# Loads tied to one another, the turns of three norms moved between products, and an S5 branch without GpSimd

## The chip, the core and the metric

The kernel runs on one core of one Trainium2 chip, in one launch. The metric is the time of an execution on the device in microseconds (us). A core has TensorE (PE in the rows: matmuls and turns, which are transposes done as matmuls), VectorE (DVE), ScalarE (ACT), GpSimd (POOL) and SyncE (SP), whose queue issues all the loads and stores here. Each engine works through its own instructions in the order in which they were written.

## The reference

One layer of an encoder over 1024 tokens of width 1024, in float32:

```python
x = layer_norm(ALPHA * x + 0.5 * swiglu(x, ffn1_w1, ffn1_w3, ffn1_w2))
proj = x @ w_in
q_lat, kv_lat, k_rope, u, g_a, g_b = split(proj)
y_a = mla_attention(q_lat, kv_lat, k_rope, ...) @ w_o_attn
y_b = s5_branch(u, f_params, b_params, d_skip, w_glu) @ w_o_ssm
x = layer_norm(ALPHA * x + (sigmoid(g_a) * y_a + sigmoid(g_b) * y_b) @ w_out)
x = layer_norm(ALPHA * x + 0.5 * swiglu(x, ffn2_w1, ffn2_w3, ffn2_w2))
ple = sigmoid(x @ ple_w_gate) * (p @ ple_w_proj)
x = layer_norm(ALPHA * x + ple)
```

`swiglu` is `(silu(x @ w1) * (x @ w3)) @ w2` with a hidden width of 2816. `s5_branch` runs a complex linear recurrence over the tokens, forwards and backwards, for 32 groups of 16 channels with 64 states each, and reads the states out with a second small matrix.

## The kernel before

Tokens stand as 8 blocks of 128 (`j`) or two halves of 512 (`h`). A float32 product is done as three: both operands are split into a high part, written by ScalarE, and a remainder, by VectorE (`split`, L63; names end in `hi`/`h` and `lo`/`l`), and `mm3` (L80) multiplies high by high, high by low and low by high, with 512 columns each. Weights come through `load_raw` (L67) into four `raw` buffers and are split into three buffers each of tags `uh` and `ul` (`wload`, L72).

**The two FFNs.** Up and down products go by seven block products in the manner of Strassen. `ffn_up` stores its seven blocks of hidden values to DRAM (`hd`). `ffn_down` (L345) works through seven stages, in the order 1, 5, 6, 3, 7, 2, 4; in each it loads six pieces of `hd` (`raw<-hd`), splits them (`hh`, `hl`) with the pieces of `w2` (`wh`, `wl`) and multiplies into `pd` or `pdy`. Its weights `w2w` and `w2e` are fetched by stage (`fetch`), and all that may be fetched early is issued as soon as its buffers are free. The residual `acc` and the norm's parameters `ln` are loaded right after.

**The norms.** In stage 4, `norm_in` (L183) takes a token block at a time: `layer_norm` (L113) sums squares on ScalarE (`scr`), takes the root, and applies the two halves of the formula with two VectorE instructions (L131 and L133). TensorE then turns the block (`tln`, L146), and `split` writes it to `xhi` and `xlo`. Turns lag the norms by three blocks (`lag`), the last norm's by two; what is left is turned by `finish`, after the first slabs of the following product have begun. A turn that is `late` goes in two tiles of four 128x128 turns through the four `pdn` buffers of PSUM; others are one tile of eight.

**Input projections.** The slabs of `w_in` (128 output columns each, 48 matmuls over both halves) follow: after the first norm the first two of four slabs of `u` (`begin`, `us[:2]`), the first half of the tokens ahead of `finish`; then the other two, six slabs of latents with the sums for their RMS norms (`pms`, `rXr`, `rXi`), and eight of the sixteen gate slabs, all under the name `pg`. `ud` holds u in DRAM; 32 loads bring it back as `U`.

**S5** (`s5_branch`, L1032) runs beside the latents and the gates. `gen` (L1249) makes, for four groups of channels, the readout weights `V`, the input weights `W` (turned on TensorE: `pw`), a Toeplitz block `K` (`pkx`, to DRAM and back as `M`) and tables `Cw`, `Sw` of cosines and sines, made from `T1` and `T2`. `scan` (L1302) multiplies `U` by `W` (`pe`), rotates by `C` and `S`, runs eight `tensor_tensor_scan` instructions into `Xr` and `Xi`, and rotates back. `read_out` (L1339) makes `py` from `M`, `Xr` and `Xi`. There are eight such iterations. GpSimd does: the products and sums of `Cw`, `Sw`, the two sums after the first rotation, and the forward half (64 partitions) of the sums after the second; VectorE does the backward half with reversed columns, and copies `bb` into `bdr`, `bdi`. In steady state 96 `pg` matmuls stand between an iteration's `pe` and the next.

**FFN2 and the end.** `first2` (L924) multiplies rows 0 and 1 of the first up products (`plain`, 96 matmuls), then calls `finish` for four blocks of the second norm, whose turns go through `tcl`, `tch`, `td`. After the third norm, `pgate` and `pproj` make the per-layer embedding, a token block at a time.

The order on each engine is set by a scheduler that works with costs of its own, subject to the data and to the pools' buffers.

Of the kernel before, what the change touches and what calls it, by code (L numbers as in the profile page):

```python
# [20 lines left out]
F32 = mybir.dt.float32  # L21
F32R = mybir.dt.float32r
# [23 lines left out]
def layer_kernel(ctx, tc, A):  # L46
# [19 lines left out]

    def load_raw(src, n=1024):  # L67
        raw = wts.tile([128, n], F32, tag="raw", bufs=RAW, name="raw")
        nc.sync.dma_start(raw, src)
        return raw  # L70

    def wload(src, tag="u", pool=None, bufs=None, n=1024):  # L72
        pool = pool or wts
        raw = load_raw(src, n)
        hi = pool.tile([128, n], F32R, tag=tag + "h", bufs=bufs, name="whi")
        lo = pool.tile([128, n], F32R, tag=tag + "l", bufs=bufs, name="wlo")
        split(raw, hi, lo)
        return hi, lo
# [104 lines left out]
    def norm_in(steps, acc, gt, bt, xT, pool, done=None, lag=3, blocks=False):  # L183


        ready = []

        def bring(late):
            j = ready.pop(0)
            if blocks:  # L190
                transpose_blocks(acc, j, xT)
            else:
                transpose_in(acc[j], j, xT, late)
            if done:
                done(j)

        def finish():
            while ready:
                bring(True)

        for j, sums in steps:
# [142 lines left out]

    def ffn_down(fp, acc, hd, w2, homes):  # L345

# [3 lines left out]
        def block(i, q):  # L350
            p, n = DUOS[q]
            t, o = (W[i], p) if p < 8 else (ends[i[0]], 3 * i[1] + p - 8)
            return t[:, o:o + n, :]

        def fetch(i):
            if i[0] not in ends:
                ends[i[0]] = homes["end", i[0]]("w2e", F32)
            W[i] = homes[i]("w2w", F32)
            for q in range(len(DUOS)):
                p, n = DUOS[q]  # L360
                nc.sync.dma_start(block(i, q), w2[i[0], i[1]][:, p:p + n, :])

        X = [pdn.tile([128, 512], F32, tag="dn", name="pd") for _ in range(4)]
        yt = []
        count = {}

# [17 lines left out]
        for i, bank, fresh, reads in stages:  # L384
            if i in want:
                fetch(want[i])
# [5 lines left out]
            for q, (p, n) in enumerate(DUOS):  # L392
                h = load_raw(hd[i - 1][q].rearrange("p a b -> p (a b)")[:, 0:n * 512], n * 512)
                w = block(right[i], q)
# [70 lines left out]
    with tc.tile_pool(name="f1", bufs=1, reuse_waits="tile") as fp:  # L465
# [80 lines left out]
        homes = {(0, 0): fx, ("end", 0): fx, (0, 1): xx, (1, 1): xx, ("end", 1): xx, (1, 0): xx}  # L546
        dn = ffn_down(fp, acc, hd, A["ffn1_w2"], homes)
        for j in range(8):
            nc.sync.dma_start(acc[j], tok(A["x"])[j])

# [3 lines left out]
        first = next(dn)  # L554
        ln = ln_params(fx("ln", F32, (128, 2, 1024)), A["ln1_g"], A["ln1_b"])
        x1T = xtiles()
        finish = norm_in(chain([first], dn), acc, *ln, x1T, fp, spill)
        us = [("w_u", m, AF.Copy, ud) for m in range(4)]
        state = begin(us[:2])
        finish()  # L560

# [362 lines left out]
    def first2():  # L924
# [33 lines left out]
        def ends():  # L958
# [12 lines left out]

    dn = ffn_down(fp, acc, hd, A["ffn2_w2"], {(0, 0): xx, ("end", 0): xx, (0, 1): xx, (1, 1): xx,
                                               ("end", 1): x16, (1, 0): x16})
    for j in range(8):
        nc.sync.dma_start(acc[j], x2d[j])
# [56 lines left out]
def s5_branch(tc, A, ud, zd, keep, pool, dram, pdn, idt):  # L1032
# [216 lines left out]
    def gen(t):  # L1249
# [47 lines left out]
        C_, S_ = tile([4, 8, 16], "Cw"), tile([4, 8, 16], "Sw")  # L1297
        cmul(C_, S_, (x(T2[0]), x(T2[1])), (y(T1[0]), y(T1[1])), g2, G)
        CS = [o.rearrange("p s a b -> p s (a b)") for o in (C_, S_)]
        return Vf, WT, M, CS  # L1300

    def scan(t, ops):  # L1302
# [20 lines left out]
        tt(t3[:, :, h], t3[:, :, h], t4[:, :, h], SUB, G)  # L1323
        X = x1, x3 = tile([4, 128], "Xr"), tile([4, 128], "Xi")
# [139 lines left out]
```

## Time and profile before

| | us |
|---|---|
| three runs: lowest, median, highest | 2364.59, 2369.57, 2371.45 |
| profiled execution | 2375.43 |
| its span, first to last instruction | 2373.6 |
| TensorE busy | 2280.4 |
| VectorE, ScalarE, GpSimd busy | 1586.0, 938.4, 390.2 |

The profile is of one execution. A row `A <- B` under waits means that A's engine sat idle until B was done. The granted clock of TensorE is given as a share: 1.00 is 2.4 GHz, 0.50 is 1.2 GHz; its mean over the span is 0.982. Durations of consecutive VectorE or TensorE instructions overlap a little, so that their starts tell the pace.

### The profile page before, as it was taken

To read this page: it belongs to the slowest core of one execution; us is meant where nothing else is said; L and a number is where in the kernel's file an instruction comes from. 1 tells how busy PE (TensorE), PEld (TensorE's weight loads), DVE (VectorE), ACT (ScalarE), POOL (GpSimd) and SP (SyncE) were. 2 spreads that over 40 slices of the span, in tenths; PEclk is the share of its full clock that TensorE was granted. 3 is DMA by queue.
4 is the path that set the end of the run, shared out by engine and by line. 5 is a ranking of instruction groups with operands and counts; after the bars stand their busy time and mean duration, and the time that the engine had idled before them with its cause. 6 is when DMAs were issued, how large, how long until landed. Compare 5 with 4: busy or idle time off the path is not lost.

```text
span 2373.6 us, 28494 instructions
## 1 busy us (share of the span) xinstructions
PE 2280.4 (96%) x10784; PEld 1876.8 (79%) x10784; DVE 1586.0 (67%) x2388; ACT 938.4 (40%) x1344; POOL 390.2 (16%) x419
## 2 busy tenths in 40 slices
PE   8999999999989989998999999989999999999897
PEld 7888888777768778886888888778888888777686
DVE  7565646665667899948688876665655646664836
ACT  5333333333432322234477871234333333233525
POOL 0000000000009455515255542000000000000000
PEclk9999999999999989998999999989999999999999
DMA  4332323932234222344100025122323327622211
GB/s 158 109 106 94 123 77 124 358 120 91 97 133 151 95 65 91 114 157 182 52 10 26 29 113 190 36 80 76 124 86 107 115 92 266 235 94 98 90 40 72
DMA packets 103899, 265.63 MB, mean 112 GB/s; under 512 B 13264, under 2 KB 27856, under 8 KB 103760
## 3 DMA queue, kind: packets, MB, share of 16 engines
q1 hardware_dynamic: 103760, 263.80, 32.3%
q8 instruction: 85, 1.39, 0.2%
q14 instruction: 54, 0.44, 0.1%
HBM read 189.33 MB, written 74.42 MB: 111 GB/s over the span
## 4 chain that ended last, share of the span: by engine, by line
PE 83%; DVE 7%; DMA 4%; issue 2%; ACT 2%; POOL 1%; SPq 0%; DVEq 0%; ACTq 0%; POOLq 0%
PE px L232 18%; PE pg L84 11%; PE py L232 9%; PE pdy L412 8%; PE pd L412 7%; PE pz L232 5%; PE pd L84 3%; PE pgate L84 3%; PE ps L84 3%; PE pov L706 2%; PE pu L270 2%; PE pg L270 2%; PE tpp L693 2%; PE pya L84 2%; DMA w2w<-in_ffn_w_dram 2%
## 5 line engine op out<-in xcount | busy, mean ns | idle before, releaser
L65 DVE TENSOR_TENSOR wlo<-raw,whi 128x1024 fp32r<-128x1024 f32 (+4 forms) x116 | 145.0, 1255 | 68.8 <-ACT whi L64 66.1
L64 ACT ACTIVATE whi<-raw 128x1024 fp32r<-128x1024 f32 (+4 forms) x116 | 112.3, 974 | 187.0 <-PE pg L84 111.4
L84 PE MATMUL pg<-xhi,whi 128*128 128x512 f32 x416 | 164.1, 395 | 0.1
L84 PE MATMUL pg<-xlo,whi 128*128 128x512 f32 x416 | 163.6, 393 | 0.3 <-DVE t L1201 0.3
L84 PE MATMUL pg<-xhi,wlo 128*128 128x512 f32 x416 | 162.9, 392 | 0.0
L412 PE MATMUL pd<-wl,hh 128*128 128x512 f32 x352 | 142.9, 406 | 6.0 <-DVE wl L65 6.0
L412 PE MATMUL pd<-wh,hl 128*128 128x512 f32 x352 | 140.9, 404 | 0.0
L412 PE MATMUL pd<-wh,hh 128*128 128x512 f32 x352 | 123.6, 404 | 7.5 <-ACT hh L64 6.6
L64 ACT ACTIVATE wh<-w2w 128x1024 fp32r<-128x1024 f32 x56 | 59.3, 1058 | 168.2 <-PE pd L412 84.2
L1232 POOL MEMSET T1r<- 128x32 f32 x1 | 0.2, 160 | 652.9 <-DMA x1d<-acc 652.9
L232 PE MATMUL py<-tch,fhl 128*128 128x512 f32 x320 | 106.0, 392 | 0.0
L412 PE MATMUL pdy<-wl,hh 128*128 128x512 f32 x264 | 104.4, 395 | 0.0
L412 PE MATMUL pdy<-wh,hl 128*128 128x512 f32 x264 | 103.9, 395 | 0.0
L65 DVE TENSOR_TENSOR hl<-raw,hh 128x1024 fp32r<-128x1024 f32 x84 | 94.9, 1132 | 11.3 <-ACT hh L64 11.2
L412 PE MATMUL pdy<-wh,hh 128*128 128x512 f32 x264 | 100.0, 396 | 0.0
L232 PE MATMUL px<-td,thi 128*128 128x512 f32 x320 | 98.8, 390 | 0.0
L64 ACT ACTIVATE fhl<-raw 128x512 fp32r<-128x512 f32 x40 | 25.3, 633 | 179.9 <-PE px L232 177.3
L65 DVE TENSOR_TENSOR wl<-w2w,wh 128x1024 fp32r<-128x1024 f32 x56 | 68.4, 1221 | 39.1 <-ACT wh L64 38.9
L680 POOL TENSOR_SCALAR P<-P,sm 128x1024 f32<-128x1024 f32 x64 | 74.8, 1170 | 117.1 <-DVE sm L679 98.4
L65 DVE TENSOR_TENSOR pt<-tpp,pt 128x512 fp32r<-128x512 f32 x128 | 85.6, 684 | 11.7 <-ACT pt L64 10.3
L84 PEld LDWEIGHTS pg<-xhi,whi 128*128 128x128 f32 x416 | 78.5, 189 | 17.2 <-issue 1.0
L84 PEld LDWEIGHTS pg<-xlo,whi 128*128 128x128 f32 x416 | 78.6, 189 | 16.8 <-DVE xlo L65 0.8
(431 smaller groups left out, 6395.0 us busy)
## 6 DMA issues: line engine op xcount, KB each, us to landing
raw<-in_ffn_w_dram SPq DMA_DIRECT2D x86, 512.0 KB, 3.7
raw<-hd SPq DMA_DIRECT2D x70, 512.0 KB, 3.3
hd<-c SPq DMA_DIRECT2D x88, 256.0 KB, 3.6
w2w<-in_ffn_w_dram SPq DMA_DIRECT2D x32, 512.0 KB, 8.6
hd<-s SPq DMA_DIRECT2D x60, 256.0 KB, 3.3
rawx<-in_xT_dram SPq DMA_DIRECT2D x16, 256.0 KB, 6.4
w2e<-in_ffn_w_dram SPq DMA_DIRECT2D x8, 512.0 KB, 8.8
acc<-in_x_dram SPq DMA_DIRECT2D x8, 512.0 KB, 8.8
```

Source lines behind the costliest of these rows:

```text
L64: S.activation(hi, src, AF.Copy)
L65: V.tensor_tensor(out=lo, in0=src, in1=hi.bitcast(F32), op=ALU.subtract)
L84: PE.matmul(out, lhsT=a, rhs=b, start=(n == 0), stop=(n == last))
L232: PE.matmul(out, lhsT=x[:, ks], rhs=y[:, k, :], start=(first and n == 0), stop=(n == 11), skip_group_check=True)
L270: PE.matmul(o, lhsT=x[:, ks], rhs=b[y][:, k, :], start=(i == 0 and k == 0 and m == 0), stop=(i == 1 and k == 3 and m == 2), skip_group_che ...
L412: PE.matmul(P[t], lhsT=x[:, ts], rhs=y[:, ws], start=(fresh and p + a == 0 and m == 0), stop=(p + a == NP - 1 and m == 2), skip_group_chec ...
L680: G.tensor_scalar(out=P, in0=P, scalar1=sm, scalar2=1.0, op0=ALU.mult, op1=ALU.mult)
L693: PE.transpose(tp[:, k * 128:k * 128 + 128], P[:, (q * 4 + k) * 128:(q * 4 + k) * 128 + 128], idt)
L706: PE.matmul(p[:, 0:256], lhsT=vt[:, k, c0:c0 + 128], rhs=pt[k // 4][b][:, k % 4, :], start=(k == 0 and b == 0), stop=(k == 7 and b == 1))
L1232: G.memset(T[0][:, :, 0], 1.0)
```

## The change

Six parts:

1. **Tied loads.** In `ffn_down`, each fetch of `w2` is issued behind a load of `hd`: the next stage's weights after this stage's third piece. The first `hd` piece of a stage is loaded ahead, at the end of the stage before; `acc` is loaded in stages 1 and 5, and `ln` behind the eighth last `hd` load. The tie is one of order on SP's queue, not a wait for the data.
2. **First norm.** The lag is four. Four slabs of `u` for the first half of the tokens (`pu`, 96 matmuls) stand ahead of `finish`, whose 32 turns come all after them; then the four slabs for the second half. The fourth slab's weights use buffers of tag `v`.
3. **u before S5.** So all of `u` is stored (8 stores `ud<-ou`) before the latents.
4. **S5 without GpSimd.** `Cw`, `Sw` and all sums go to VectorE in full width; ScalarE copies the forward rows of `Xr`, `Xi` and, reversed, the backward rows, and copies `bb` into `bdr`, `bdi`. `Vi` is made with a negated `c`, which takes away one negation per iteration. The making of `T1`, `T2` and the RMS work stay on GpSimd.
5. **first2.** `finish(2)` after row 0, and again between the parts of row 1.
6. **Third norm.** The lag is four, and `finish` comes when the gate products reach block 4.

```diff
-    def ffn_down(fp, acc, hd, w2, homes):
+    def ffn_down(fp, acc, x0, hd, w2, homes, hs):
...
+        def behind(load):
+            if hs:
+                with tc.issue_after(hs[-1].ins):
+                    load()
+            else:
+                load()
...
-            if i in want:
+            if i == 1:
                 fetch(want[i])
...
-                h = load_raw(hd[i - 1][q].rearrange("p a b -> p (a b)")[:, 0:n * 512], n * 512)
+                if q == 0:
+                    h = ahead or hload(i, 0)
+                else:
+                    h = hload(i, q)
+                if q == len(DUOS) - 1 and i != 4:
+                    ahead = hload(follows[i], 0)
+                if q == 2 and i != 4 and follows[i] in want:
+                    fetch(want[follows[i]])
+                if q == 4 and i in (1, 5):
+                    for j in range(4):
+                        behind(lambda: nc.sync.dma_start(acc[j + (i == 5) * 4], x0[j + (i == 5) * 4]))
...
-        us = [("w_u", m, AF.Copy, ud) for m in range(4)]
-        state = begin(us[:2])
-        finish()
+        us = [wload(A["w_u"][m]) if m < 3 else wload(A["w_u"][m], "v", fp, 4) for m in range(4)]
+        for h in range(2):
...
+            for w, p in zip(us, ps):
+                up(p, w, x1T, h)
+            if h == 0:
+                finish()
...
-        for row, s in ((0, s1), (1, s2)):
-            for _ in plain(X2b, w, 0, row, s[:, l]):
-                pass
-        finish()
+        for _ in plain(X2b, w, 0, 0, s1[:, l]):
+            pass
+        finish(2)
+        for _ in plain(X2b, w, 0, 1, s2[:, l]):
+            finish(2)
...
-        cmul(C_, S_, (x(T2[0]), x(T2[1])), (y(T1[0]), y(T1[1])), g2, G)
+        cmul(C_, S_, (x(T2[0]), x(T2[1])), (y(T1[0]), y(T1[1])), g2, V)
...
-        tt(t1[:, :, h], t1[:, :, h], t2[:, :, h], ADD, G)
+        tt(t1[:, :, h], t1[:, :, h], t2[:, :, h], ADD, V)
...
-            tt(o[fw], x[fw], y[fw], op, G)
-            tt(o[bw, :, ::-1], x[bw], y[bw], op, V)
+            tt(x, x, y, op, V)
+            S.activation(o[fw], x[fw], AF.Copy)
+            S.activation(o[bw, :, ::-1], x[bw], AF.Copy)
```

**SP's queue at the end of FFN1's up products.** Before (w2w, w2e: weights of the down product; hd: stores and loads of the hidden values):

```order
107 L361 DMA w2w<-in_ffn_w_dram 128x1024 x4
108 L361 DMA w2e<-in_ffn_w_dram 128x1024
109 L361 DMA w2e<-in_ffn_w_dram 128x512
110 L69 DMA raw<-hd 128x1024
111 L361 DMA w2e<-in_ffn_w_dram 128x1024
112 L361 DMA w2e<-in_ffn_w_dram 128x512
113 L361 DMA w2w<-in_ffn_w_dram 128x1024 x8
114 L320 DMA hd<-s_2788 128x512
115 L361 DMA w2e<-in_ffn_w_dram 128x1024
116 L361 DMA w2e<-in_ffn_w_dram 128x512
117 L361 DMA w2w<-in_ffn_w_dram 128x1024 x4
118 L361 DMA w2e<-in_ffn_w_dram 128x1024
```

With the change:

```order
107 L367 DMA w2w<-in_ffn_w_dram 128x1024 x4
108 L367 DMA w2e<-in_ffn_w_dram 128x1024
109 L367 DMA w2e<-in_ffn_w_dram 128x512
110 L367 DMA w2e<-in_ffn_w_dram 128x1024
111 L367 DMA w2e<-in_ffn_w_dram 128x512
112 L69 DMA raw<-hd 128x1024
113 L367 DMA w2w<-in_ffn_w_dram 128x1024 x4
114 L323 DMA hd<-s_2788 128x512
115 L323 DMA hd<-s_2787 128x512
116 L420 DMA acc<-in_x_dram 128x1024 x3
```

Before, the weights of three stages (twelve `w2w`, six `w2e`) stand ahead of the last stores of `hd` (`s_2787`) and of everything behind them; now those of two, and the third set and half of `acc` follow stage 1's loads.

**ScalarE at the end of FFN1's down product.** Before:

```order
278 L64 ACTIVATE whi<-raw 128x1024
279 L64 ACTIVATE xhi<-tln 128x8x128
280 L121 ACTIVATE scr,ln_4510<-acc,ln_4509 128x1024
281 L64 ACTIVATE xhi<-tln 128x8x128
282 L121 ACTIVATE scr,ln_4549<-acc,ln_4548 128x1024
283 L121 ACTIVATE scr,ln_4588<-acc,ln_4587 128x1024
284 L123 ACTIVATE ln_4510<-ln_4511 128x1
285 L64 ACTIVATE whi<-raw 128x1024 x2
```

With the change:

```order
279 L64 ACTIVATE whi<-raw 128x1024
280 L64 ACTIVATE xhi<-tln 128x8x128
281 L123 ACTIVATE scr,ln_4498<-acc,ln_4497 128x1024
282 L64 ACTIVATE whi<-raw 128x1024 x2
283 L123 ACTIVATE scr,ln_4537<-acc,ln_4536 128x1024
284 L64 ACTIVATE whi<-raw 128x1024
285 L123 ACTIVATE scr,ln_4576<-acc,ln_4575 128x1024
286 L64 ACTIVATE xhi<-tln 128x8x128
```

The second `xhi<-tln` of each piece is that of block 3, the last one that the first half of the tokens needs. Before it stood behind one `scr`; now it stands behind three `scr` and three `whi<-raw`. On VectorE, `xlo` of block 3 likewise stands behind three `wlo<-raw` and the first norm instruction of blocks 4, 5 and 6.

**VectorE in one S5 iteration, the part behind the scans.** Before:

```order
835 L1066 TENSOR_TENSOR Wr<-Wr,v_7046 128x512
836 L1327 SCALAR_TENSOR_TENSOR Xi<-r_4788,t_7018 128x128 x4
837 L1066 TENSOR_TENSOR t_7016<-Xr,Cw 128x512
838 L1066 TENSOR_TENSOR t_7019<-Xr,Sw 128x512
839 L1066 TENSOR_TENSOR v_7046<-PW_4779,bb_re 128x512
840 L1066 TENSOR_TENSOR t_7017<-Xi,Sw 128x512
841 L1066 TENSOR_TENSOR t_7018<-Xi,Cw 128x512
842 L1066 TENSOR_TENSOR Wi<-Wi,v_7046 128x512
843 L1066 TENSOR_TENSOR Xr<-t_7016,t_7017 64x4x128
844 L1066 TENSOR_TENSOR Xi<-t_7018,t_7019 64x4x128
```

With the change:

```order
901 L1104 TENSOR_TENSOR t_7296<-Xr,Cw 128x512
902 L1104 TENSOR_TENSOR t_7299<-Xr,Sw 128x512
903 L1104 TENSOR_TENSOR t_7297<-Xi,Sw 128x512
904 L1104 TENSOR_TENSOR t_7298<-Xi,Cw 128x512
905 L65 TENSOR_TENSOR wlo<-raw,whi 128x1024
906 L1104 TENSOR_TENSOR v_7328<-PW_4966,bb_re 128x512
907 L1104 TENSOR_TENSOR t_7296<-t_7296,t_7297 128x512
908 L1104 TENSOR_TENSOR Sw<-T2r,T1i 128x512
909 L1104 TENSOR_TENSOR t_7298<-t_7298,t_7299 128x512
910 L1104 TENSOR_TENSOR Cw<-T2r,T1r 128x512
911 L1104 TENSOR_TENSOR Wi<-Wi,v_7328 128x512
912 L1104 TENSOR_TENSOR Cw<-Cw,v_7329 128x512
```

Two half-width sums (64x4x128) became two full ones (`t<-t,t`, 128x512), and the products and sums of `Cw` and `Sw` (six per iteration) now stand among VectorE's instructions. On TensorE the `pg` matmuls between one iteration's `pe` and the next went from 96 to 83 in most iterations, one has 78; behind the last `pe` 41 stand ahead of the readout, where 48 stood.

## Rows read from the trace of the kernel before

**Rows 1.** Busy time by stretch: length, then each engine (count), granted clock, DMA share, GB/s.
```profile
426.50:468.87 42.37, 42.37 (x184) 34.14 (x182) 30.09 (x32) 11.08 (x14) 0.00 (x0) 1.00 1.03 413
...
470.97:477.80 6.83, 6.08 (x14) 4.79 (x15) 6.12 (x9) 4.75 (x5) 0.00 (x0) 0.50 1.03 419
...
2037.69:2041.10 3.41, 3.41 (x9) 2.63 (x9) 2.64 (x3) 3.14 (x4) 0.00 (x0) 0.50 1.03 422
827.85:836.20 8.35, 5.11 (x26) 4.65 (x26) 8.18 (x10) 0.00 (x0) 8.19 (x9) 0.80 0.21 65
853.39:866.92 13.53, 7.72 (x33) 6.91 (x33) 11.94 (x15) 3.28 (x6) 7.36 (x8) 0.62 0.22 76
1583.72:1597.37 13.65, 11.51 (x33) 8.69 (x34) 12.24 (x21) 3.34 (x5) 0.00 (x0) 0.50 0.00 1
672.44:686.01 13.57, 3.22 (x13) 2.96 (x13) 13.57 (x36) 6.31 (x13) 0.40 (x1) 0.62 0.41 153
2236.29:2253.00 16.71, 10.95 (x42) 7.81 (x41) 15.87 (x39) 10.05 (x17) 0.00 (x0) 0.80 0.38 126
```

**Rows 2.** Waits of PE over 468 to 475 us: line, releaser, us in total, times, longest.
```profile
PE pd L412 <- ACT hh L64: 2.9, 1, 2.9
```

**Rows 3.** Waits of PE over 2030 to 2040 us.
```profile
PE pd L412 <- ACT hh L64: 3.8, 1, 3.8
```

**Rows 4.** DMA issues over 430 to 475 us: count, KB each, median us to landing.
```profile
w2w<-in_ffn_w_dram SPq DMA_DIRECT2D x12, 512.0 KB, 9.3
```

**Rows 5.** Waits of PE over 672 to 700 us.
```profile
PE tln L146 <- DVE ln L128: 10.4, 1, 10.4
```

**Rows 6.** ACT groups over 672 to 700 us: count, busy us, mean ns, idle before.
```profile
L121 ACT ACTIVATE scr<-acc,ln 128x1024 bf16<-128x1024 f32 x3 | 3.4, 1136 | 0.0
L64 ACT ACTIVATE xhi<-tln 128x512 fp32r<-128x512 f32 x6 | 3.3, 601 | 11.0 <-PE tln L146 11.0
L64 ACT ACTIVATE whi<-raw 128x1024 fp32r<-128x1024 f32 x2 | 2.0, 1046 | 0.0
```

**Rows 7.** DVE over 672 to 690 us, in time: start, us, line, tile, count.
```profile
674.15 1.28 DVE L131 SCALAR_TENSOR_TENSOR acc<-acc,ln,ln 128x1024 f32<-128x1024 f32 x1
...
676.79 2.34 DVE L65 TENSOR_TENSOR wlo<-raw,whi 128x1024 fp32r<-128x1024 f32 x2
```

**Rows 8.** Waits of PE over 800 to 875 us.
```profile
PE pw L1270 <- DVE Wr L1066: 5.1, 1, 5.1
PE py L1346 <- DVE Xr L1066: 2.9, 1, 2.9
PE pw L1270 <- DVE Wi L1066: 1.4, 2, 0.8
PE py L1344 <- DMA M<-kd: 1.0, 1, 1.0
```

**Rows 9.** DVE groups over 875 to 1025 us: count, busy us, mean ns, idle before.
```profile
L1066 DVE TENSOR_TENSOR Vi<-Vi,v 128x512 f32<-128x512 f32 x5 | 7.0, 1394 | 0.0
...
L1066 DVE TENSOR_TENSOR t<-pe,Cw 128x508 f32<-128x508 f32 x10 | 6.7, 673 | 1.7 <-PE pe L1311 1.7
```

**Rows 10.** DVE over 824 to 828 us, in time.
```profile
824.94 0.68 DVE L1066 TENSOR_TENSOR t<-Xi,Sw 128x512 f32<-128x512 f32 x1
825.54 0.68 DVE L1066 TENSOR_TENSOR t<-Xi,Cw 128x512 f32<-128x512 f32 x1
```

**Rows 11.** The stretch 875 to 1025 us, columns as in Rows 1.
```profile
875.00:1025.00 150.00, 150.00 (x896) 128.15 (x896) 142.10 (x196) 44.20 (x55) 78.64 (x60) 1.00 0.32 99
```

**Rows 12.** PE groups over 875 to 1025 us: count, busy us, mean ns.
```profile
L84 PE MATMUL pg<-xhi,wlo 128*128 128x512 f32 x166 | 64.9, 391 | 0.0
```

**Rows 13.** Waits of PE over 1550 to 1595 us.
```profile
PE tln L162 <- DVE tcl L65: 4.1, 2, 3.6
```

**Rows 14.** Waits of PE over 2230 to 2280 us.
```profile
PE pgate L84 <- DVE wlo L65: 2.3, 2, 1.5
PE pgate L84 <- ACT whi L64: 2.0, 1, 2.0
```

More of the change, by code (lines that the diff above doesn't have):

```diff
@@ L65, in split, with load_raw @@
         V.tensor_tensor(out=lo, in0=src, in1=hi.bitcast(F32), op=ALU.subtract)
-    def load_raw(src, n=1024):
+    def load_raw(src, n=1024, note=None):
         raw = wts.tile([128, n], F32, tag="raw", bufs=RAW, name="raw")
-        nc.sync.dma_start(raw, src)
+        dma = nc.sync.dma_start(raw, src)
+        if note is not None:
+            note.append(dma)
         return raw
@@ L195, in bring, with finish @@
                 done(j)
-        def finish():
-            while ready:
+        def finish(n=8):
+            while ready and n:
                 bring(True)
+                n -= 1
         for j, sums in steps:
@@ L360, in fetch, with hload @@
                 p, n = DUOS[q]
-                nc.sync.dma_start(block(i, q), w2[i[0], i[1]][:, p:p + n, :])
-        X = [pdn.tile([128, 512], F32, tag="dn", name="pd") for _ in range(4)]
-        yt = []
-        count = {}
+                behind(lambda: nc.sync.dma_start(block(i, q), w2[i[0], i[1]][:, p:p + n, :]))
+        def behind(load):
[4 more added lines that the diff above has]
+                load()
+        X = [pdn.tile([128, 512], F32, tag="dn", name="pd") for _ in range(4)]
+        follows = {1: 5, 5: 6, 6: 3, 3: 7, 7: 2, 2: 4}
+        ahead = None
+        def hload(i, q):
+            n = DUOS[q][1] * 512
+            return load_raw(hd[i - 1][q].rearrange("p a b -> p (a b)")[:, 0:n], n, hs)
         def add(out, j, n, ps, first, last):
@@ L402, in ffn_down @@
                 held.append((p, n, hh, hl, wh, wl))
+                if i == 4 and 0 < q < 5:
+                    yield q - 1, sums[q - 1]
                 if i == 4 and q == 4:
@@ L546, in layer_kernel @@
         homes = {(0, 0): fx, ("end", 0): fx, (0, 1): xx, (1, 1): xx, ("end", 1): xx, (1, 0): xx}
-        dn = ffn_down(fp, acc, hd, A["ffn1_w2"], homes)
-        for j in range(8):
-            nc.sync.dma_start(acc[j], tok(A["x"])[j])
+        hs = []
+        dn = ffn_down(fp, acc, tok(A["x"]), hd, A["ffn1_w2"], homes, hs)
         def spill(j):
@@ L554, in layer_kernel @@
         first = next(dn)
-        ln = ln_params(fx("ln", F32, (128, 2, 1024)), A["ln1_g"], A["ln1_b"])
+        with tc.issue_after(hs[-8].ins):
+            ln = ln_params(fx("ln", F32, (128, 2, 1024)), A["ln1_g"], A["ln1_b"])
         x1T = xtiles()
-        finish = norm_in(chain([first], dn), acc, *ln, x1T, fp, spill)
-        us = [("w_u", m, AF.Copy, ud) for m in range(4)]
-        state = begin(us[:2])
-        finish()
+        finish = norm_in(chain([first], dn), acc, *ln, x1T, fp, spill, 4)
+        us = [wload(A["w_u"][m]) if m < 3 else wload(A["w_u"][m], "v", fp, 4) for m in range(4)]
+        for h in range(2):
+            if h == 0:
+                ps = [t[:, c:c + 512] for t in [pup.tile([128, 1024], F32, tag="up", name="pu") for _ in range(2)]
+                      for c in (0, 512)]
+            else:
+                ps = [pdn.tile([128, 512], F32, tag="dn", name="pu") for _ in range(4)]
+            for w, p in zip(us, ps):
+                up(p, w, x1T, h)
+            if h == 0:
+                finish()
+            for m, p in enumerate(ps):
+                o = fp.tile([128, 512], F32, tag="s", bufs=2, name="ou")
+                S.activation(o, p, AF.Copy)
+                nc.sync.dma_start(ud[m][:, h * 512:h * 512 + 512], o)
     def latents(ev, tp):
@@ L970, in layer_kernel @@
     acc = [fa.tile([128, 1024], F32, tag="a", bufs=8, name="acc") for _ in range(8)]
[L972 to L975, printed above, removed]
+    hs = []
+    dn = ffn_down(fp, acc, x2d, hd, A["ffn2_w2"], {(0, 0): xx, ("end", 0): xx, (0, 1): xx, (1, 1): xx,
+                                               ("end", 1): x16, (1, 0): x16}, hs)
     first = next(dn)
-    gt, bt = ln_params(x16("ln", F32, (128, 2, 1024)), A["ln3_g"], A["ln3_b"])
+    with tc.issue_after(hs[-8].ins):
+        gt, bt = ln_params(x16("ln", F32, (128, 2, 1024)), A["ln3_g"], A["ln3_b"])
     x3T = [[f(n) for _ in range(2)] for f, n in ((xx, "xhi"), (x16, "xlo"))]
-    finish = norm_in(chain([first], dn), acc, gt, bt, x3T, fp, lag=2)
+    finish = norm_in(chain([first], dn), acc, gt, bt, x3T, fp, lag=4)
     gt, bt = ln_params(x16("ln", F32, (128, 2, 1024)), A["ln4_g"], A["ln4_b"])
```

23 lines of the change are left out of this document (12 added, 11 removed).

## The prediction

> **What bounds the kernel now.** I read the span and the busy times first: TensorE is busy for 2280.4 of 2373.6 us, so the kernel is bound by its matmuls, and only what TensorE loses can be won. Then I took TensorE's waits stretch by stretch, and the granted clock of the same stretches. [rows 1] is to be read this way: where a stretch has the clock 0.50 throughout, TensorE was at 1.2 GHz, and half of its busy time there is lost on top of the idle time. In every one of these stretches the clock fell after an idle gap, never in the full ones (the first row: 42.37 of 42.37 us busy, clock 1.00). So an idle gap costs twice, and a change that moves no matmul away must show as smaller gaps. The losses that the change touches, idle and clock:
>
> - Entry of FFN1's down product: 2.9 us [rows 2], then 6.08 us busy at half clock, of which half is lost [rows 1]: 2.9 + 3.0 = 5.9. FFN2's: 3.8 [rows 3] and 3.41 / 2 [rows 1]: 5.5.
> - After the first norm: 10.4 idle [rows 5], then 3.22 us busy at half clock [rows 1]: 12.0.
> - S5's start: 5.1 + 2.9 + 1.4 + 1.0 = 10.4 idle [rows 8]. Two stretches of [rows 1] show its clock: 8.35 us at 0.80 means 3.3 us at half clock, all of it busy, 1.7 lost; 13.53 at 0.62 means 10.3 at half clock, with all 7.72 busy us in it, 3.9 lost. Together 16.0.
> - FFN2's first products: 4.1 idle [rows 13] and 11.51 / 2 = 5.8 from the clock [rows 1]: 9.9.
> - Behind the third norm: 16.71 - 10.95 = 5.8 idle, and 0.20 x 2 x 16.71 = 6.7 us at half clock, mostly busy, some 2.8 lost [rows 1]: 8.6.
>
> **The change part by part.**
>
> *Tied loads.* At 426.5 to 468.87 the DMA share is 1.03 at 413 GB/s [rows 1]: everything issued there stands in line, and a weight block takes 9.3 us to land [rows 4]. The late `hh` of [rows 2, 3] waits for `hd` loads at the end of this line. Before, three sets of weights, `ln` and `acc` stood ahead of them (12 x 0.5 MB in `w2w` alone); the order now puts two sets and half of `acc` there: about 5.5 + 2 MB instead of 8.3 + 4 + 1, some 5.8 MB less, 14 us at 413 GB/s. The last `hd` piece, 3 us late, comes early. The third set then comes under the first stages, where the products last longer than its 7 us. I take the whole 5.9 + 5.5 = **-11.4**; bounds -11.4 and, if the last stores of `hd` set the time and not the line, -5.
>
> *First norm.* Here the order speaks against a gain. The 96 `pu` matmuls may start when block 3 is in `xhi` and `xlo`. Count from T, the end of the last `pd`. ScalarE has two `whi`, whose buffers the last products free, one `scr`, one `whi`, one `scr` ahead: 3 x 1.05 + 2 x (1.14 + 0.19 for reading the sum), then `xhi`, about 1.0 [rows 6]: T + 6.8. VectorE has three norm instructions of 1.28 and three `wlo` of 1.17 ahead [rows 7], plus a last sum and small ones, about 1.2, then `xlo` with 1.2: T + 9.7. The second matmul of `pu` already reads `xlo`. TensorE has block 3's eight turns to do, 1 us, so it idles about 8.7 instead of 10.4, with the clock lost as before and more busy time in it (2.4 instead of 1.6). The 32 turns behind come in eight late tiles; each takes ScalarE 0.60 [rows 6] and four buffers are there, so with the copy of the last `pu` ahead the last `xhi` is written some 5.4 us after that product, while the turns themselves take about 4 (13 matmuls in 3.22 us at half clock is 0.12 each at full, [rows 1]): another 1.5. Sum -1.7 + 0.8 + 1.5, about **+1**; bounds -12 (gap gone) and +4. The stores and loads of `u` that are moved ahead of the latents have some 100 us until the first `pe`, and cost nothing as long as the latents' 200-odd matmuls cover them.
>
> *S5 without GpSimd.* Beside GpSimd, VectorE's sums with two SBUF inputs take 1.39 us; those that read `pe` from PSUM take 0.67 at all times [rows 9]; where GpSimd is still, two-input ones take 0.68 and start every 0.60 [rows 10]. So the 30 products and sums of an iteration after the change cost 18 us, the eight scans 2.7, `wlo` and `K` 2.4: about 23 us. TensorE's iteration: 32 matmuls of each kind make one, so 166 in 150 us [rows 12] are 5.2 iterations of 29 us; at 42.37 / 184 = 0.23 each [rows 1], 13 fewer between make it 26. VectorE, busy for 142.1 of 150 us before [rows 11], gets air although its list is longer. With that the late `Wr`, `Xr` and `Wi` of [rows 8] come in time: behind the first `pe` the order leaves 65 `pg` and 28 small matmuls, about 19 us, before `Xr` is read; VectorE and ScalarE need about 15.5. At the end it gets worse: 41 instead of 48 `pg` cover the last chain (10 products and sums at 0.60, scans 2.7, two copies of 0.6 at the end: 11 us against 9.4), about +1. I leave 1.5 for waits that stay. Sum -16.0 + 1 + 1.5 = **-13.5**; bounds -17 and, if only the waits for GpSimd's own results go, -4.
> The Trainium skill (SBUF — State Buffer, section Who interferes with whom) says that a VectorE instruction with two SBUF inputs and a GpSimd instruction that reads SBUF block each other for a whole instruction, while one with at most one SBUF input is left alone. The trace agrees: 1.39 against 0.67. By that rule no such pair ever ran together, and moving GpSimd's half over gives up no overlap.
>
> *first2.* Four turns at a time between parts of plain products give `tcl` and `td` a time of 36 matmuls, 8 us, to be written. The gaps go, and the clock with them: 9.9 less some 0.4 that stays: **-9.5**; bounds -11 and -4.
>
> *Third norm.* Turning block 3 behind the last `pd`, with three `whi` in a row, leaves one wait of about 2.2 us for the second `wlo` (VectorE writes it behind `xlo` and a norm instruction) where 2.3 + 2.0 stood [rows 14]; the 32 late turns cost about 2 as above, the clock about 1. 8.6 becomes 5.2: **-3.5**; bounds -8.6 and +2.
>
> Matmuls are neither added nor taken away. Sum: -11.4 + 1 - 13.5 - 9.5 - 3.5 = -36.9. The profiled execution, 2375.43 us with 1.8 outside its span, lies 5.9 above the median of 2369.57. From 2375.4 it goes to 2338.5, which for the median means **2332.7**.
>
> **The rivals.**
>
> *A: VectorE becomes the bound of S5 (slower).* If its sums are slow for another reason than GpSimd, the moved ones are slow too. Before, an iteration cost VectorE 142.1 / 5.2 = 27.5 us; without the negation, the half-width sums and the copies about 20.5. Ten more at 1.39 make 34.4 against TensorE's 26: 8.4 lost in each of eight iterations, +67, and the start's 13.5 isn't won. 2332.7 + 13.5 + 67 = 2413. It decides as soon as the mean pace of the 30 passes 0.70 us. For it: VectorE was near full. Against: [rows 9, 10]. Chance 0.04.
>
> *B: the first norm's gap closes.* If block 3 is written before the queued work that I count, 12 us go instead of +1: 2320. Against it stands the order on ScalarE and VectorE. Chance 0.12.
>
> *C: S5 keeps its late start.* The copies of `Xr`, `Xi` stand on ScalarE behind table loads and an `og` that waits for a slab's end; if they come 3 to 5 us later than I count, the gaps and the clock loss stay, and only 4 is won: 2342. Together with a first2 that keeps its clock loss: 2348. Chance 0.16.
>
> *D: the down entries wait on for the last `hd` stores*, and the ties do little: -5 instead of -11.4, so 2339. Chance 0.10.
>
> *E: most gaps return elsewhere*, as the next late thing takes each place (`raw` loads, `M`, the first norm): under 7 us are left, about 2366. Chance 0.04.
>
> **How the numbers follow.** The forecast gets what remains, 0.54, and is 2332.7. Its own bounds are not all met at once: about 12 either way. B and full gains reach 2314, C with a bad first norm 2354; these are the ends of the range, and A, E and corners lie outside it. A measurement of this kernel can tell about 0.3%, 7 us, from no change. Faster by more: forecast, B, C, D, 0.92. Within it: E, 0.04. Slower: A, 0.04.
>
> **What would show it.** Right: no wait over 1 us and a clock of 1.00 at the two down entries, with a DMA share there well below 1.03 in the last 20 us; a gap of 8 to 9 us behind the first norm, ended by `xlo`; S5 iterations of about 26 us in which VectorE's two-input sums take 0.68; first2 without the stretch at 0.50. Wrong: sums on VectorE above 0.70 in pace with GpSimd still, waits for `Xr` of several us, or a first norm under 3 us idle.

## The result, and the profile after

The change took the kernel from 2367.93 us (median of four runs on the same chip, 2364.59 to 2371.45) to **2340.28 us** (2339.93 to 2342.82): a ratio of 0.9885, 95% interval 0.9868 to 0.9903. The forecast was 2332.7, its range 2314 to 2354. The sign and the range held. The sum of terms came close partly by luck: one wait that no step had foreseen ate what other places gave beyond their forecast.

The profiled execution of after took 2340.56 us, at its own median, with a span of 2338.7; that of before, 2375.43, stood 7.5 above this median of 2367.93. So between the two profiles 34.9 us went, between the medians 27.7. TensorE's busy time went from 2280.4 to 2260.9, its mean clock from 0.982 to 0.991. Six places that both traces have, each the start of the same wait on TensorE (the last is the span's end), show where; the lead is how much earlier after reaches the place:

| place | before | after | lead | gained since the place above |
|---|---|---|---|---|
| FFN1's down product, `pd<-wl,hh` | 641.84 | 636.20 | 5.6 | 5.6 |
| behind S5, first wait at `pglu<-zs,whi` | 1061.56 | 1054.65 | 6.9 | **1.3** |
| attention, `pov<-pt,vt` | 1223.92 | 1211.37 | 12.6 | 5.6 |
| start of FFN2, `pu<-xah,whi` | 1554.19 | 1541.58 | 12.6 | 0.0 |
| FFN2's down product, `pd<-wl,hh` | 2205.67 | 2176.54 | 29.1 | 16.5 |
| end of the span | 2373.6 | 2338.7 | 34.9 | 5.8 |

The stretch of the first norm, `u` and S5, on which parts 2 to 4 of the change work, gained next to nothing. TensorE's waits of after, four stretches one behind the other (columns as in [rows 2]):

```profile
PE pu L86 <- ACT xhi L64: 5.3, 1, 5.3
PE pu L86 <- DVE xlo L65: 2.5, 1, 2.5
PE tln L148 <- DVE xlo L65: 0.7, 1, 0.7
...
PE pms L625 <- DVE rXr L65: 12.3, 1, 12.3
...
PE py L1390 <- DMA M<-kd: 1.3, 1, 1.3
PE pw L1315 <- DVE Wr L1104: 0.8, 1, 0.8
...
PE pgate L86 <- DVE wlo L65: 2.2, 1, 2.2
PE tln L148 <- DVE xlo L65: 1.5, 2, 1.1
PE pgate L86 <- ACT whi L64: 0.4, 1, 0.4
```

The first two stand for [rows 5], and come to 7.8 us where the forecast said 8.7; the third is a wait at the late turns. The two rows with `M` and `Wr` are all that is left of the four in [rows 8]. The row between is new: 12.3 us at the first `pms`, the sum over squares of a latent slab for its RMS norm. Before has no wait there. The stretches of after by engine (columns as in [rows 1]):

```profile
448.40:468.40 20.00, 20.00 (x88) 16.22 (x87) 15.60 (x16) 5.62 (x8) 0.00 (x0) 1.00 0.96 379
...
780.00:798.00 18.00, 5.65 (x15) 3.98 (x14) 8.64 (x14) 4.86 (x7) 11.66 (x40) 0.62 0.07 29
...
830.00:1020.00 190.00, 188.71 (x1158) 161.43 (x1157) 168.90 (x303) 81.99 (x125) 6.93 (x18) 1.00 0.33 98
...
1560.00:1600.00 40.00, 40.00 (x203) 33.35 (x203) 26.35 (x37) 12.87 (x17) 0.00 (x0) 1.00 0.16 54
...
1988.90:2008.90 20.00, 20.00 (x87) 16.21 (x87) 15.60 (x16) 5.62 (x8) 0.00 (x0) 1.00 0.97 374
```

Over the 20 us up to the place in each down product where before waited for `hh` (first and fifth row), TensorE is full at clock 1.00, and no wait for `hh` follows. The DMA share there is 0.96 and 0.97, little below the 1.03 of [rows 1]: the queue is still nearly full, and what changed is the order on it. ScalarE writes the `hh` that before waited for 13 us earlier, first in before, then in after:

```profile
471.04 0.63 ACT L64 ACTIVATE hh<-raw 128x512 fp32r<-128x512 f32 x1 [1.31 <-DMA raw<-hd]
...
458.10 0.61 ACT L64 ACTIVATE hh<-raw 128x512 fp32r<-128x512 f32 x1
```

The turns of first2 (fourth row), which [rows 1] had at 0.50, run full at 1.00. S5 (third row) runs at 1.00 with 1.3 us idle in 190, and GpSimd is busy for only 6.9 us of it. The second row is the new loss: 12.35 idle, then 5.65 us busy, of which 5.1 us are at half clock, so 2.6 more: 15.0 in all. What stands behind it, followed back through after, engine by engine (start, us, line, tile, count, idle before and releaser):

```profile
726.93 0.42 SPq L1090 DMA_DIRECT2D c_re<-in_c_re_dram  x1
727.89 0.43 SPq L1194 DMA_DIRECT2D t<-in_lam_re_dram  x1
...
734.88 0.26 POOL L1104 TENSOR_TENSOR t<-t 128x32 f32<-128x32 f32 x1 [34.77 <-DVE t L1104]
...
791.41 0.24 POOL L1104 TENSOR_TENSOR Xr<-Xr,t 128x32 f32<-128x32 f32 x1
...
791.69 0.63 ACT L617 ACTIVATE rt<-og 128x512 f32<-128x512 f32 x1 [21.44 <-POOL Xr L1104]
...
788.94 0.72 DVE L1104 TENSOR_TENSOR Cw<-T2r,T1r 128x512 f32<-128x512 f32 x1 [13.18 <-POOL T2r L1104]
...
792.13 0.68 DVE L65 TENSOR_TENSOR rXr<-rt,rt 128x512 fp32r<-128x512 f32 x1
...
792.87 0.80 PE L625 MATMUL pms<-rXr,ones 128*128 128x512 f32 x1 [12.35 <-DVE rXr L65]
```

SP issues the loads of S5's parameters at 727 to 728; GpSimd starts the tables `T1`, `T2` at 735 and needs 57 us for them; their scratch is tagged `Xr`, and so is the buffer that the RMS work takes next; ScalarE's `rt<-og`, VectorE's `rXr` and TensorE's `pms` follow within 2 us of the last table instruction. The same rows of before:

```profile
686.84 0.45 SPq L1052 DMA_DIRECT2D c_re<-in_c_re_dram  x1
688.10 0.48 SPq L1156 DMA_DIRECT2D t<-in_lam_re_dram  x1
...
704.33 0.26 POOL L1066 TENSOR_TENSOR t<-t 128x32 f32<-128x32 f32 x1 [17.57 <-DVE t L1066]
...
764.85 0.63 ACT L577 ACTIVATE rt<-og 128x512 f32<-128x512 f32 x1 [7.51 <-POOL Xr L1066]
```

and before's instructions on the tile `pms` (count, shortest, median and longest in ns, first and last start):

```profile
L585 PE MATMUL pms<-rXr,ones x2: 392/396/401, 774.9 to 797.8; 128*128 128x512 f32 x2
```

The parameters were issued 40 us earlier, the tables began 31 and ended 27 us earlier. ScalarE waited for the scratch there too, 7.5 us, but TensorE had other work and came to this `pms` at 774.9, 10.05 us behind `rt<-og`, which needs 1.18 to get there (791.69 to 792.87 in after). So the slack was 8.9 us; TensorE comes 5.6 us later in after (780.5), and 26.8 - 8.9 - 5.6 is the wait of 12.3. These rows were in the trace of before, and the forecast did not use them.

On SP's queue the parameter loads wait for nothing of their own. They stand behind the stores `ud<-ou`, and SP's waits from 680 to 740 us in after are mostly those of these stores for `ou` (39.7 us). That the loads stand there because of the memory of `u`'s buffers is an inference; C, D and E change the buffers and see where the loads go.

### The profile page after: what moved, and what is told of

Same layout as the page of the kernel before. It is cut to its first block, busy times and chain, and to the rows that moved or that the text cites. A ratio compares the mean times of both kernels' runs of the same rounds, so it can differ in the third digit from the quotient of the medians.

```text
span 2338.7 us, 28503 instructions
## 1 busy us (share of the span) xinstructions
PE 2260.9 (97%) x10784; PEld 1862.5 (80%) x10784; DVE 1547.1 (66%) x2416; ACT 968.9 (41%) x1417; POOL 269.5 (12%) x339
## 4 chain that ended last, share of the span: by engine, by line
PE 48%; DVE 4%; ACT 2%; issue 1%; DMA 0%; POOL 0%; SPq 0%; DVEq 0%; ACTq 0%
PE px L235 9%; PE py L235 5%; PE pd L441 4%; PE pdy L441 4%; PE pd L86 3%; PE pgate L86 3%; PE ps L86 3%; PE pz L235 2%; PE pov L746 2%; PE tpp L733 2%; PE pya L86 2%; PE pyb L86 2%; PE pq L86 1%; PE pu L273 1%; PE pg L273 1%; PE pg L86 1%
## 5 line engine op out<-in xcount | busy, mean ns | idle before, releaser
L65 DVE TENSOR_TENSOR wlo<-raw,whi 128x1024 fp32r<-128x1024 f32 (+4 forms) x116 | 139.0, 1203 | 64.6 <-ACT whi L64 61.9
L86 PE MATMUL pg<-xhi,whi 128*128 128x512 f32 x352 | 139.0, 395 | 0.0
L86 PE MATMUL pg<-xlo,whi 128*128 128x512 f32 x352 | 138.5, 394 | 0.0
L86 PE MATMUL pg<-xhi,wlo 128*128 128x512 f32 x352 | 138.4, 393 | 0.0
L249 DVE TENSOR_TENSOR c<-raw 128x512 f32<-128x512 f32 x40 | 27.5, 688 | 93.9 <-PE px L235 93.9
L86 PE MATMUL ps<-k,qh 96*128 96x512 f32 (+1 forms) x256 | 84.3, 408 | 3.2 <-ACT P L718 1.8
L441 PEld LDWEIGHTS pd<-wl,hh 128*128 128x128 f32 x352 | 66.3, 188 | 24.1 <-DVE wl L65 9.1
```

Of the source, the lines that this page charges most:

```text
L65: V.tensor_tensor(out=lo, in0=src, in1=hi.bitcast(F32), op=ALU.subtract)
L86: PE.matmul(out, lhsT=a, rhs=b, start=(n == 0), stop=(n == last))
L249: V.tensor_tensor(out=c[:, r], in0=r2[:, l], in1=r2[:, r], op=ALU.add)
L441: PE.matmul(P[t], lhsT=x[:, ts], rhs=y[:, ws], start=(fresh and p + a == 0 and m == 0), stop=(p + a == NP - 1 and m == 2), skip_group_chec ...
```

## The experiments

Ratios are against runs of before on the same chip; the medians of before lay between 2368.26 and 2369.49. The expectations speak of `Xr` and `pms` as above.

### What the wait at `pms` consists of

**A. First product of the tables on GpSimd.**

```diff
-        cmul(C_, S_, (x(T2[0]), x(T2[1])), (y(T1[0]), y(T1[1])), g2, V)
+        cmul(C_, S_, (x(T2[0]), x(T2[1])), (y(T1[0]), y(T1[1])), g2, G if t == 0 else V)
```

> Edit: Cw and Sw of the first S5 iteration go back to GpSimd; all else as in the change. Theory M (the S5 parameters arrive about 40 us later than before because the second half of u still holds buffers whose place the S5 tiles take; so GpSimd's tables end about 27 us later): VectorE no longer waits for the tables, but ScalarE's squares of the latents share buffers with the tables' scratch, so the wait of 12.4 us moves from the first pms pair to the second, to about 8 to 12 us: 2338 to 2342 us. Rival Q (only the place of Cw in VectorE's queue delays rXr): the wait and the clock loss behind it go: about 2325 us.

Measured: 2347.08 us (2341.12 to 2353.78), 0.9914 [0.9891, 0.9937]. That is 6.8 above the change: TensorE waits 13.9 us at the same `pms`, and 4.2 us for `Xr` at S5's end, which the change does not have. VectorE around the end of the first wait:

```profile
792.72 1.53 DVE L65 TENSOR_TENSOR rXr<-rt,rt 128x512 fp32r<-128x512 f32 x1 [16.00 <-POOL Xr L1104]
794.18 1.76 DVE L619 TENSOR_TENSOR rt<-rt,rt 128x512 f32<-128x512 f32 x1
```

`Cw` no longer stands ahead of `rXr`, and `rXr` comes no earlier: it waits for the scratch itself. So it was not VectorE's order; and the wait did not pass to a later `pms` either, as I had thought the other outcome would be. GpSimd now makes part of `Cw` between its last table instructions, which ends the tables 1 us later. With GpSimd multiplying beside them, these two instructions take 1.53 and 1.76 us where after has 0.68 for the same.

**B. The tables on VectorE.** `T1` and `T2` are made with `V` in place of `G`.

> Edit: the tables T1 and T2 and the powers they need are made on VectorE instead of GpSimd; parameters arrive as late as in the change. Theory M: some 100 small instructions of 0.2 to 0.3 us, about 20 to 25 us on VectorE where GpSimd took 50 (735 to 792); rXr comes near 780 and the wait shrinks from 12.4 to 0 to 5 us: 2326 to 2333 us. Rival: VectorE is too full there and the wait stays over 8 us: 2337 us or more.

Measured: 2340.04 us, 0.9886 [0.9871, 0.9901], no change against after. The wait at `pms` is gone, and two others stand in its place:

```profile
PE py L1392 <- ACT Xr L1382: 6.1, 2, 5.9
PE pg L86 <- ACT og L479: 5.4, 1, 5.4
```

A faster maker of the tables takes the wait away, which says that their end set it; but the loss returns at 811 us (`og`) and at S5's end, 1018 us (`Xr`). The expectation had the wait and the time fall together, or neither. That VectorE is then too full is my reading, not shown.

**C. Three slabs of u, and no buffer of the FFN in the second half.** The fourth slab goes with the latents; results leave through the raw weight buffers.

```diff
-        us = [wload(A["w_u"][m]) if m < 3 else wload(A["w_u"][m], "v", fp, 4) for m in range(4)]
+        us = [wload(A["w_u"][m]) for m in range(3)]
...
-                o = fp.tile([128, 512], F32, tag="s", bufs=2, name="ou")
+                o = wts.tile([128, 1024], F32, tag="raw", bufs=RAW, name="raw")
...
+    project(sp, [("w_u", 3, AF.Copy, ud)])
```

> Edit: the first norm is covered by three slabs of u instead of four, their results leave through raw buffers, and the fourth slab comes with the latents, so that no buffer of the first FFN is held by u's second half. Theory M: the S5 parameters are issued some 20 us earlier, the tables end before VectorE asks for them, and the 12.4 us wait at pms goes with its clock loss of about 2.6: 2325 us, or up to 2329 if the fourth slab's weights come 2 to 4 us late. Rival Q: Cw still stands ahead of rXr, and the wait stays: about 2340.

Measured: 2325.58 us (2324.49 to 2328.68), 0.9827 [0.9810, 0.9843]: 14.7 below after, where the wait and its clock are worth 15.0. SP and GpSimd:

```profile
687.42 5.76 SPq L600 DMA_DIRECT2D ud<-raw  x3
693.23 0.42 SPq L1091 DMA_DIRECT2D c_re<-in_c_re_dram  x1
...
701.77 0.26 POOL L1105 TENSOR_TENSOR t<-t 128x32 f32<-128x32 f32 x1 [7.49 <-DVE t L1105]
```

The parameters are issued 34 us earlier, the tables start 33 us earlier, and TensorE has no wait at `pms`. It has another of 4.8 us instead, for the fourth slab's `whi`, with a stretch at half clock behind it (0.92 over 700 to 745 us). That 14.7 equals the price of the wait so nearly is therefore chance: the first norm's waits fell from 8.5 to 6.8 us too, and S5's own (`M`, `Wr` and, at its end, `Xi`, 2.9 us) are gone.

**D and E. Which buffer holds the parameters.** In D the change has only its results moved to the raw buffers, in E only the fourth slab's weights moved (C with the results back in tag `s`). D:

```diff
-                o = fp.tile([128, 512], F32, tag="s", bufs=2, name="ou")
+                o = wts.tile([128, 1024], F32, tag="raw", bufs=RAW, name="ou")
```

> The change with one edit: the results of u on the way out go through the raw weight buffers in place of the buffers of S5's parameters; the fourth slab's weights stay where the change has them (the buffers tagged v). Theory, the v buffers of the fourth slab hold the parameters too: they are still issued late (near 725 us), the pms wait stays at 9 to 13 us, about 2337 to 2341 us. Rival, the buffers of the results alone hold them: parameters near 690 us, no pms wait, about 2326 us as the run with three slabs and free buffers gave.

> As the run with three slabs and free buffers, but the results of u go out through the two buffers tagged s, as the change has it; so only the fourth slab's v buffers are taken away. With the run before it, this tells which of the two holds the S5 parameters. Theory, each of the two holds them by itself: the parameters come only behind the sixth store of u, near 715 us (the changed kernel 727, the run with both freed 693), the tables end some 10 us earlier than in the change, and a wait at or behind the first pms of 1 to 5 us is left: about 2330 us (2325 to 2335). Rival, the v buffers alone hold them: parameters near 693 us, no wait, about 2326 us or, since the latents' first weights are loaded earlier, 2319.

Measured, D: 2351.47 us, 0.9928 [0.9911, 0.9945]; E: 2336.49 us (2335.11 to 2337.36), 0.9869 [0.9842, 0.9896]. TensorE's waits in D:

```profile
PE pms L625 <- DVE rXr L65: 11.6, 1, 11.6
PE pg L86 <- ACT whi L64: 9.9, 1, 9.9
```

SP and ScalarE in E, in time, and TensorE's wait there:

```profile
717.11 0.32 SPq L600 DMA_DIRECT2D ud<-ou  x1
718.27 0.46 SPq L1091 DMA_DIRECT2D c_re<-in_c_re_dram  x1
...
784.26 0.63 ACT L617 ACTIVATE rt<-og 128x512 f32<-128x512 f32 x1 [16.82 <-POOL Xr L1105]
```

```profile
PE pms L625 <- DVE rXr L65: 13.2, 1, 13.2
```

In both the parameters stay late: in D `c_re` is issued at 722.7, but the load of `lam_re`, from which the tables start, only behind the last store at 728.3 (727.9 in after); in E `c_re` is issued at 718.3, against 693.2 in C. Each of the two tags holds them by itself, and only freeing both helps. My times were off in both. In D the results take raw buffers that the latents' first weights had, hence 9.9 us more at `pg`. In E the tables end 7.4 us earlier than in after, but with some 40 matmuls less ahead of it TensorE also comes to `pms` 8.3 us earlier (772.2 in place of 780.5), so the wait is as long as it was. What counts is the distance between the two, which I had not subtracted.

**F. The change with u as before**: two slabs ahead of the first norm, the others behind it, lag three; all other parts as changed.

> The change with the projection of u as the kernel before has it (two slabs ahead of the first norm, the others in the late turns as before); the tied loads, the S5 part, first2 and the third norm stay as changed. Theory, the four other parts add up and only the new order of u costs: about 2319 us (2315 to 2324), from the time of before less 10.3 (tied loads), 16.5 (first2 and third norm) and 22.3 (S5), each as its single run gave it. The S5 parameters are issued near 685 us, the wait at the first pms of S5 (12.35 us in the changed kernel) is gone, the first norm's gap is 10.4 us with the clock window behind it as before. Rival, the parts take from one another and the order of u is not what ate the gain: 2330 us or more, with gaps elsewhere.

Measured: **2322.90 us** (2322.29 to 2324.74), 0.9803 [0.9789, 0.9818]. The wait at `pms` is gone, `c_re` is issued at 679.61, and the first norm's wait is the old one:

```profile
PE tln L148 <- DVE ln L130: 10.3, 1, 10.3
```

So parts 2 and 3 of the change, taken together, cost 17.4 us (19 by the ratios).

### What the other parts are worth

**G. S5's part alone, on the kernel before.**

> Edit: the kernel before with the S5 part of the change alone (Cw, Sw and all sums on VectorE, copies on ScalarE). The forecast's term: the waits for Wr, Xr, Wi go with the clock loss, 13.5 us less than before: about 2354. Rival A (VectorE's sums stay slow without GpSimd and it becomes the bound): at or above 2368. Rival Q: Cw on VectorE waits for GpSimd's tables here too, and holds back rXr by several us: 2358 to 2368.

Measured: 2345.97 us (2339.37 to 2352.68), 0.9909 [0.9885, 0.9933], 22.3 less than before; its runs differ by 13 us, and the interval is about 6 us either way. From 700 to 1030 us TensorE is busy for 330.00 of 330 us at clock 1.00 and waits for nothing that the profile lists, so all of the 16.0 that the forecast had found there is gone. The start of the attention also lost less, though nothing in it was edited: its stretch in the table above, 162.4 us long in before, lasts 155.5 here, and the wait for `ckl` is 4.0 us in place of 6.4.

**H. The loads as before, in the changed kernel.**

> Edit: the change with the loads of both down products as before (all weights as early as their buffers allow, then acc and ln). The forecast's term: 11.4 us are given back, 2.9 and 3.8 us of waiting for hh and the clock loss behind them, so about 2351 us. Rival: the entries were won by something else, the waits stay away: about 2340.

Measured: 2350.56 us (2348.09 to 2354.75), 0.9925 [0.9906, 0.9944], 10.3 more than the change. Both waits of [rows 2, 3] are back, and the clock with them (0.83 over 470 to 480 and over 2014 to 2024 us):

```profile
PE pd L415 <- ACT hh L64: 2.8, 1, 2.8
...
PE pd L415 <- ACT hh L64: 3.6, 1, 3.6
```

**I. first2 and the third norm as before, in the changed kernel.**

> Edit: the change with first2 as before (all four turns after both rows) and the third norm's lag at two again. The two stand 450 us apart, so that the trace reads each by itself. The forecast's terms: the first products of FFN2 lose 9.5 us again (a stretch at 0.50 with some 11 us busy, gaps of 5 us), the end of the third norm 3.5 (5.8 us idle instead of 2 to 4): about 2353 us. Rival: the waits were tied to the late S5 or to the loads: 2340 to 2345.

Measured: 2356.82 us (2355.11 to 2357.95), 0.9949 [0.9933, 0.9965], 16.5 more than the change. The waits of [rows 13, 14] return, and the clock behind them (columns of [rows 2], then of [rows 1]):

```profile
PE tln L164 <- DVE tcl L65: 4.1, 2, 3.6
...
PE pgate L86 <- DVE wlo L65: 2.3, 2, 1.6
PE pgate L86 <- ACT whi L64: 2.0, 1, 2.0
```

```profile
1571.00:1585.00 14.00, 10.60 (x31) 7.97 (x32) 13.50 (x23) 3.93 (x6) 0.00 (x0) 0.51 0.00 0
2220.00:2235.00 15.00, 9.51 (x34) 6.99 (x34) 13.80 (x34) 7.96 (x14) 0.00 (x0) 0.72 0.48 140
```

G, H and I add up to 22.3 + 10.3 + 16.5 = 49.1; F, which has all three, is 46.6 below its before. So these parts take little from one another, as far as G's spread lets one say.

### What is left, and a faster version

**J. Block 3 first.** In the changed kernel the splits of slabs 2 to 4 are put behind block 3's `xhi` and `xlo` in the order.

```diff
+        a, v = splits
+        us = [wload(A["w_u"][0])]
+        with tc.issue_after(a.ins), tc.issue_after(v.ins):
+            us += [wload(A["w_u"][m]) if m < 3 else wload(A["w_u"][m], "v", fp, 4) for m in range(1, 4)]
```

> Edit: the splits of the second to fourth slab's weights are ordered behind those of token block 3. Theory of the order (xhi and xlo of block 3 stand behind three whi and three wlo): the idle time behind the first norm falls from 8.6 to about 5 us: 2336 us. Rival: the second slab's wlo then comes late, or the norm instructions alone hold xlo: idle time within 1 us of 8.6, 2340 us.

Measured: 2338.37 us (2337.39 to 2340.99), 0.9874 [0.9854, 0.9894]; 1.9 less than the change, though the runs of the two overlap. The waits behind the norm:

```profile
PE pu L88 <- ACT xhi L66: 2.4, 1, 2.4
PE pu L88 <- DVE xlo L67: 2.2, 1, 2.2
```

They come to 4.6 us where 7.8 stood, so the weights' splits ahead of block 3 were worth 3 us; three squares (`scr`) still stand ahead of `xhi` on ScalarE.

**K. C and J together**, with the fourth slab's weights loaded early, and the loads of `U` behind the latents' third weights.

> Edit: the three-slab version with block 3 first as in the run beside it, the fourth slab's weights loaded with the others, and the loads of U ordered behind the third load of latent weights. Theory M: no wait at pms, the 4.8 us wait of the three-slab version for the fourth slab's whi and its clock loss of 2.5 go, and some 3.4 us behind the first norm: about 2315 us. Rival: the held raw buffer makes the latents' weights late in their turn: 2320 to 2326.

Measured: **2318.82 us** (2318.16 to 2320.24), 0.9790 [0.9774, 0.9806], faster than both kernels: 49.9 less than before, 21.5 less than the change, 4.1 less than F, and between the theory's 2315 and the rival's 2320. The waits from 655 to 1030 us, but for one of 0.2:

```profile
PE pu L91 <- ACT xhi L66: 2.4, 1, 2.4
PE pu L91 <- DVE xlo L67: 2.2, 1, 2.2
PE pms L633 <- ACT rt L66: 1.5, 1, 1.5
```

## Why the prediction was right, and where it was not

- **Tied loads** (-11.4): right. -5.6 at FFN1's entry, forecast -5.9; H measures both as 10.3. Rival D, which would have kept the waits, is out: there is none left at either entry. The sign that the forecast named, a DMA share well below 1.03 over the last 20 us, hardly came (0.96 and 0.97): the loads needed first came earlier in a line that stayed nearly full.
- **First norm** (+1): right in its walk through the queues, 7.8 us idle against 8.7, ended by `xhi` and `xlo` as said, and J shows that the weights' splits counted there are real. The clock was low for 10.2 us there, 5.6 of them busy, so 2.8 were lost to it; with 0.7 of a wait at the late turns, where the forecast had 1.5, the place costs 11.3 against 12.0 before. So it gained 0.7 instead of losing 1. Rival B, that the gap closes, is out.
- **S5** (-13.5): right. VectorE's sums with two SBUF inputs fell from the 1394 ns of [rows 9] to 680, and six iterations' rotations fit where five did:

```profile
L1104 DVE TENSOR_TENSOR t<-pe,Cw 128x508 f32<-128x508 f32 x12 | 8.1, 678 | 2.7 <-PE pe L1356 2.7
...
L1104 DVE TENSOR_TENSOR Vi<-Vi,v 128x512 f32<-128x512 f32 x6 | 4.1, 680 | 0.0
```

  These are VectorE's groups of after over 866 to 1016 us, as long as the stretch of [rows 9]: 12 halves in 150 us are 25 us an iteration, forecast 26. Rival A, VectorE as the bound, would have needed a pace above 0.70 and is out. The rule of the Trainium skill (SBUF — State Buffer, section Who interferes with whom) agrees from both sides here: without GpSimd 680 ns, and in A, with GpSimd brought back for one product, 1.53 and 1.76 us. Within the change S5's own losses went from the 16.0 us of the forecast's count to 2.1, a gain of 13.9; the extra 1 us that the forecast saw at S5's end did not come (a wait of 0.7 for `Xi` in before, 0.8 in after).
- **The step that failed** is the sentence "The stores and loads of `u` that are moved ahead of the latents have some 100 us until the first `pe`, and cost nothing as long as the latents' 200-odd matmuls cover them." It followed the moved stores to the consumer of their data and no further. It did not ask what stands behind them: the loads of S5's parameters, whose place the buffers of `u` (tags `v` and `s`) held until the last slab was done. They came 40 us later, the tables ended 27 us later. The chain had 8.9 us to spare. The cost is 15.0 us in the trace; C, which has the wait no more, is 14.7 below the change and F 17.4, each with smaller differences besides. Rivals C and E were about late starts in S5 and about losses that return elsewhere, but neither had this wait, nor its size.
- **first2 and third norm** (-9.5 and -3.5): right in kind, 3.5 us short in sum (16.5 in I). In I's trace 11.3 us of the loss stand at first2 and 4.3 behind the third norm. At first2 the forecast left out two waits for `td` of 0.7 and 0.6 us, which before and I have and after has not. The third norm's stretch gave 5.8 in the table, but 1.7 of that is no work of the change: behind a gap of 2.0 us in FFN2's down product before has a clock of 0.88 over 2207.6 to 2222 us, where after has 1.00.
- **Unforeseen gain**: 5.6 us at the start of the attention, which no part edits. Its waits came to 12.0 us in place of 14.1, and the mean clock to 0.98 in place of 0.95. G, with S5's part alone, gains 6.9 us in the same stretch, so that the other parts are not needed for it. Whether it comes from S5's part, or whether the one profiled execution of before was slow there, stays open.
- **The offset.** The forecast took 36.9 us off the profile, and 34.9 went. It then carried the distance of before's profiled execution to the median (5.9) over to after. Its profiled execution lies on its median; the carried distance is most of the 7.6 us by which the forecast was too low. That the unforeseen wait (15.0) was nearly made up by gains of some 13 us beyond the forecast is chance: 5.6 in the attention, 3.8 from FFN2 on, 1.7 at the first norm, 1.7 from a stretch at half clock at 645 us that before's execution had and after's had not, and 0.4 in S5, less 0.3 at FFN1's entry.

## What to carry to other kernels

When a step is moved earlier, list not only what reads its results but every tile that later takes over the memory of its buffers, and go on from those loads until a chain ends at the bounding engine; a release that another engine already waits for, even at no cost, marks a chain without slack. And compare distances: a chain that ends 7 us earlier wins nothing if the engine that waits for it arrives 8 us earlier too, as E shows.

## What the runs showed of the hardware

The same idle gap does not always cost clock. A gap of 2.0 us at 636 to 638 us in FFN1's down product, for `wl`, is in all these kernels; the stretch from 636 to 650 us in after, and then in J, at equal busy time:

```profile
636.00:650.00 14.00, 12.02 (x54) 9.60 (x54) 13.96 (x29) 7.71 (x12) 0.35 (x4) 1.00 0.42 150
```

```profile
636.00:650.00 14.00, 12.02 (x46) 9.62 (x46) 13.96 (x29) 6.32 (x11) 0.35 (x4) 0.88 0.41 150
```

J's edit lies behind this stretch, and ScalarE's instructions there have the same order in both; yet J ran part of it at half clock, with eight matmuls fewer in the same time: 0.12 of 14 us, 1.7 us, which after did not lose. A, C and F had the same gap and 1.00 too; before and the other eight runs had some 3.4 us at half clock behind it. The gap of 2.0 us for `wl` in FFN2's down product went the same two ways, 0.88 in before, 1.00 in after and in I. So a gap near 2 us carried a price of 0 or 1.7 us; what decides between the two, these runs do not show. A term built on the clock rows of one profiled execution is uncertain by about as much.
